# Three reorderings at stage borders of a two-layer conv/attention block: the gate products of the convolution, the second stream's 1/rms, and the first block pair's last sums

## The chip, the cores and the metric

The kernel runs on one core of a Trainium2 chip. The metric is the time of one execution on the device in microseconds (us), lower is better; the median of several runs is given. The engines are named as in the profile: PE is TensorE (matmuls), PEld its weight loads, DVE is VectorE, ACT is ScalarE, POOL is GpSimd, SP is SyncE, which here only issues DMAs.

## The reference, cut to what matters

Two streams of 256 tokens each, the latent `x` and the context `ctx`, of width 1024, go through two layers. Each layer is: half a gated feed-forward net (FFN), a mixer, and half an FFN again, every one behind an RMS norm with a modulation (a scale and a shift, computed from a conditioning vector) and added back through a gate. Layer 0's mixer is a short convolution, layer 1's is grouped-query attention. After layer 1's mixer only the latent stream goes on.

```python
def _rms(t, g):
    t32 = t.astype(jnp.float32)
    y = t32 * lax.rsqrt(jnp.mean(t32 * t32, axis=-1, keepdims=True) + NORM_EPS)
    return y.astype(t.dtype) * g

def _modulate(t, g, shift, scale):
    return _rms(t, g) * (1 + scale) + shift

def _swiglu(h, w13, w2):
    gte, up = jnp.split(h @ w13, 2, axis=-1)
    return (jax.nn.silu(gte) * up) @ w2

def _short_conv_mixer(h, w_in, k, w_out):
    bgate, cgate, xv = jnp.split(h @ w_in, 3, axis=-1)
    return (bgate * _dwconv3(cgate * xv, k)) @ w_out
```

## The kernel before

Activations are kept transposed: width on the 128 partitions (eight tiles k of 128, `KT = 8`), tokens along the free dimension, the latent stream in columns 0 to 255 (called s = 0) and the context stream in columns 256 to 511 (s = 1). Products keep fp32 accuracy by splitting each operand into a high part and a low rest (`split`: ACT copies the high part, DVE subtracts), and `mm3` (L133) makes three matmuls of one product: high by high, high weight by low activation, low weight by high activation. A "product" below is one such matmul, as in the description of the change. Weights come by DMA as raw fp32 tiles (`load_raw`, eight buffers `wr`), and `load_w` splits them into halves of 1024 columns (`wh`, `wl`, four buffers each).

**FFN.** 22 pairs of a gate tile and an up tile (`pg`, `pu`) are worked off in three groups (`THIRDS` = 8, 7, 7), each followed by `project`, the multiplication with the second weight. In the FFNs with both streams most pairs are done by blocks (`Pair`, with `h.blk` tiles of class `Blocks`): a scheme in the manner of Strassen with seven block products instead of eight. It needs sums of activation blocks (`Blocks.sums`: T1 to T4, high and low parts `th`, `tl`) and of weight blocks (`Pair.sums`: S1 to S4). `Pair.sums(1)` makes a copy of a weight block (`split_far`), then the subtraction at L729 and the split into S3 and S4. The block products are called in five steps: `head` (A11, A12), `five` (S1 by T1), `six` (S2 by T2, S4 by a plain block), `seven` (S3 by T3), `four` (A22 by T4).

**The borders.** The norm needs the sum of squares over all 1024 rows, so it can only start when the last tile of the stage before is done. At the end of a stage, `project` therefore does tiles 6 and 7 stream by stream: first s = 0, then s = 1. What the norm of a stream has to do is put into a list `pending` by `tail_norm`, and `flush(n)` runs the first n entries at chosen places in the program. For s = 0 these are three entries, run inside `project`. For s = 1 it is one entry, `both_parts`: `rms_sum` (two PE products with ones, L270; a square root on ACT, L275; a reciprocal `ri` on DVE, L279), `rms_all` (two PE products with the identity, L288, that spread `ri` over all partitions), and then the eight tiles of the norm itself (`scaled`, L300, and the high and low parts). The next stage begins with products of s = 0 only, so that the norm of s = 1 runs beside them.

The three kinds of border that the change touches:

- FFN to convolution (once). The convolution has three groups of products, `pv`, `pc` (weights `wcx`) and `pb` (weights `wb`, the gate b). For its first output tile, m = 0, it goes stream by stream with k outermost, three groups for each k, and calls `flush()` behind the twelfth `mm3` (n == 11).
- Into an FFN with blocks (twice: layer 0's second FFN and layer 1's first). Two plain pairs come first: pair 0 with s = 0, `flush()`, the load of pair 1's weights, pair 1 with s = 0, then `h.sums(0)`, pair 0 with s = 1, `h.sums(1)` and the first block pair's `sums(0)`, pair 1 with s = 1, the first block pair's `head`, `h.sums(2)` (T3 and T4), and the first block pair's `sums(1)` (S3 and S4). `tc.issue_after(every[-1])` keeps pair 1's products on PE behind the last product of `rms_all`.
- FFN to attention (once): a `flush()` between two projections.

**Order of instructions.** Outside the parts that are written out by hand, a planner sorts each engine's instructions before the run. It walks through time with its own estimates of durations, and when several instructions of an engine are ready it takes the one that stands first in the program. So the order in the program is a priority, not the order on the engine; a lower one is taken where the higher is not ready by the planner's estimate. `issue_after` adds a fixed order on one engine. On the chip each engine then follows the sorted order.

Of the kernel before, what the change touches and what calls it, by code (L numbers as in the profile page):

```python
# [18 lines left out]
KT = D // P  # L19
S = 256  # L20
# [27 lines left out]
def hybrid_kernel(ctx: ExitStack, tc: tile.TileContext, a: dict, out: bass.AP):  # L48
    nc = tc.nc
# [83 lines left out]
    def mm3(ps, w, m, first, last, more=False):  # L133
        wh, wl = w
        kw = {"skip_group_check": True} if more else {}
        mh, ml = m
        nc.tensor.matmul(ps, wh, mh, start=first, stop=False, **kw)  # L137
        nc.tensor.matmul(ps, wh, ml, start=False, stop=False, **kw)  # L138
        nc.tensor.matmul(ps, wl, mh, start=False, stop=last, **kw)  # L139

    def mm_wide(ps, ws, ms, first, last):

# [202 lines left out]
    class Early:  # L345
# [3 lines left out]
        w = S + 2  # L349
# [126 lines left out]
    pending = []  # L476

    def flush(n=9):
        while pending and n:
            pending.pop(0)()  # L480
            n -= 1
# [30 lines left out]
    def tail_norm(l, j, h):  # L512

        box = {}

        def tail(m, c0, c1):
            square_add(m, c0, c1)
            if m == KT - 1:
                if not box:
                    box["A"] = scale_of(l, j)  # L520
                    box["B"] = mod_ready(l, 3 * j)
                s = c0 // S

                def inv():
                    return rms_inv(s)

                def rest(part, ri, ks=range(4)):

                    if isinstance(h, Blocks):
                        h.block(s, part, box["A"], box["B"], ri, s == 0, ks)  # L530
                    else:
                        for k in ks:
                            norm_k(s, 4 * part + k, h, box["A"], box["B"], ri)

                def both_parts():
                    ri = inv()
                    for part in range(2):
                        rest(part, ri)

                if s == 0:  # L540
                    keep = []

                    def one():
                        keep.append(inv())
                        rest(0, keep[0])

                    pending.append(one)
                    pending.append(lambda: rest(1, keep[0], range(2)))
                    pending.append(lambda: rest(1, keep[0], range(2, 4)))
                else:  # L550
                    flush()
                    pending.append(both_parts)

        return tail

# [85 lines left out]
    def at13(j, k):  # L641

        return (k // 4) * 1024 + j * T2 + (k % 4) * P

    def w13_mm(pp, w, h, ks, c0, c1):
        for k in ks:
            mv = pick(h, k, c0, c1)
            for i in range(2):
                mm3(pp[i][:, c0:c1], w(at13(1 - i, k)), mv, k == 0, k == KT - 1)

    def w13_post(pp, g, c0, c1):
        n = c1 - c0
# [119 lines left out]
    def ffn(l, b, h, tot, gate, tail, gs=(), ev=(0, 0), z=None):  # L772
        gs = list(gs)
        i0 = 0
        for t, n in enumerate(THIRDS):
            between = ()
            if tot == T2:
                heads = []
                if t == 0 and not gs:

                    w = [load_w(a["w13"][l, b, 0])]
                    gs = [new_pair("g") for _ in range(2)]
                    pp = [(psum("pg"), psum("pu")) for _ in range(2)]
                    w13_mm(pp[0], w[0], h, range(KT), 0, S)
                    flush()
                    w.append(load_w(a["w13"][l, b, 1]))
                    with tc.issue_after(every[-1]):
                        w13_mm(pp[1], w[1], h, range(KT), 0, S)
                    h.sums(0)
                    w13_mm(pp[0], w[0], h, range(KT), S, T2)  # L790
                    w13_post(pp[0], gs[0], 0, T2)
                    heads.append(Pair(a["w13"][l, b, 2], h))
                    h.sums(1)
                    heads[0].sums(0)
                    w13_mm(pp[1], w[1], h, range(KT), S, T2)
                    w13_post(pp[1], gs[1], 0, T2)
                    heads[0].head()
                    h.sums(2)
                    heads[0].sums(1)
                prev = None  # L800
                for i in range(len(gs), n):
                    if t == 0 and not heads and i in AS_IS[l, b]:
                        w = load_w(a["w13"][l, b, i])
                        pp = psum("pg"), psum("pu")
                        if prev:
                            prev.seven()
                        if "T1" not in h.t:
                            with tc.issue_after(rows["W1"]):
                                h.sums()
                        w13_mm(pp, w, h, range(4), 0, T2)  # L810
                        if prev:
                            gs.append(new_pair("g"))
                            prev.four(gs[-1])
                            prev = None
                        w13_mm(pp, w, h, range(4, KT), 0, T2)
                        gs.append(new_pair("g"))
                        tick(3, w13_post(pp, gs[-1], 0, T2))
                        continue
                    if heads:
                        pr = heads.pop(0)  # L820
                    else:
                        pr = Pair(a["w13"][l, b, i0 + i], h)
                        pr.sums(0)
                        pr.sums(1)
                        pr.head()
                    pr.five()
                    at = prev.seven().ins if prev else None
                    pr.six()
                    if prev:
                        gs.append(new_pair("g"))  # L830
                        prev.four(gs[-1])
                    prev = pr
                    if i:
                        tick(0.9, at)

                def last():
                    gs.append(new_pair("g"))
                    prev.four(gs[-1])

                between = (prev.seven, last) if prev else ()  # L840
            else:
                for i in range(n):
                    w = load_w(a["w13"][l, b, i0 + i])
                    gs.append(beside(gp.tile([P, T2], F32R, name=nm("gx"), tag="gh")))
                    pp = psum("pg"), psum("pu")
                    if i0 + i < EARLY:
                        for k in range(KT):
                            for j in range(2):
                                ps = pp[j][:, : z.w]
                                mm3(ps, w(at13(1 - j, k)), z.at(k), k == 0, k == KT - 1)  # L850
                            if i == 0 and k == KT // 2:
                                flush(1)
                        if i < 3:
                            flush(1)
                        early_post(pp, gs[i], z.ri)
                        tick(1)
                        continue
                    for j in range(2):
                        ws = [w(at13(1 - j, k)) for k in range(KT)]
                        mm_wide(pp[j], ws, [h.both(k) for k in range(KT)], True, True)  # L860
                    beside_post(pp, gs[i])
                    tick(1)
            i0 += n

            def ws2(m):
                src = a["w2a"][l, b, m // 2] if t == 0 else a["w2b"][l, b, t - 1, m // 2]
                o = (m % 2) * n * P
                raw = load_raw(src[:, o : o + n * P], n * P)
                hi, lo = half()
                split(hi[:, : n * P], lo[:, : n * P], raw[:, : n * P])  # L870
                return lambda k: (hi[:, k * P : k * P + P], lo[:, k * P : k * P + P])

            cur = gs
            end = t == len(THIRDS) - 1
            project(
                ws2,
                (lambda k, c0, c1: cur[k]) if tot == S
                else lambda k, c0, c1: (cur[k][0][:, c0:c1], cur[k][1][:, c0:c1]), n,
                gate, tail if end else None, tot, 2 if end and tot == T2 else 0, ev[end], between,
            )  # L880
            gs = []
# [191 lines left out]
    h = hn  # L1073

    zs = []
    for m in range(KT):
# [4 lines left out]
        for c0, c1 in ((0, S), (S, T2)) if m == 0 else ((0, T2),):  # L1081
            groups = ((pv, wcx, P), (pc, wcx, 0), (pb, wb, (m % 2) * P))
            if m == 0:
                order = [(k, *g) for k in range(KT) for g in groups]
            else:
                order = [(k, *g) for g in groups for k in range(KT)]
            for n, (k, ps, w, off) in enumerate(order):
# [397 lines left out]
```

## Time and profile before

| | |
|---|---|
| median of 3 runs | 1556.71 us (1556.70 to 1556.72) |
| the profiled execution | 1558.75 us; its span, first to last instruction, 1557.0 us |
| PE busy | 1545.5 us, 99% of the span, 10252 matmuls |
| DVE, ACT, POOL busy | 82%, 50%, 14% |
| granted TensorE clock, mean | 0.999 |
| DMA | 263.5 MB, 169 GB/s mean |

The profiled execution took 2.04 us more than the median, and 1.75 us of it lie outside the span. PE is the engine that sets the end: what matters are the places where it stood still. A matmul's end in the profile is modelled, and neighbours overlap: a matmul over 256 columns has a duration of 0.28 us, while the next one starts 0.12 us after it. So the loss at a wait is read from the starts: the distance of two starts less the usual distance.

### The profile page before, as it was taken

What the parts mean: (1) busy time and instruction counts of PE and PEld (TensorE: products, weight loads), DVE (VectorE), ACT (ScalarE), POOL (GpSimd) and SP (SyncE); (2) the same over time, 40 slices, a digit from 0 to 9 for tenths busy, and PEclk for the clock granted to TensorE, in tenths of its full rate; (3) what the DMA queues carried; (4) which work ended last, traced back from release to release, by engine and by line L of the source; (5) the groups of instructions that cost most, each with busy time, mean ns of one, the idle gap of its engine ahead of it and who ended that gap; (6) DMA issues with size and microseconds to landing.
All of it is one profiled execution on the core that took longest, in us unless ns stands there. A gap on an engine that the chain in (4) does not pass through costs nothing.

```text
span 1557.0 us, 26280 instructions
## 1 busy us (share of the span) xinstructions
PE 1545.5 (99%) x10252; PEld 1416.9 (91%) x10252; DVE 1284.5 (82%) x2003; ACT 781.9 (50%) x1297; POOL 221.8 (14%) x187
## 2 busy tenths in 40 slices
PE   9999999999999999999999999999999999999999
PEld 7898998998888899989999899989999899998888
DVE  5789799799987489978979888968978888898676
ACT  5642553544322366436446476436446455774553
POOL 0012212200000012032032012022042002300000
PEclk9999999999999999999999999999999999999999
DMA  9557477475565424655656634655767843266562
GB/s 368 197 167 197 115 186 203 111 199 166 187 204 178 115 62 121 207 142 146 199 149 153 205 77 123 203 156 133 220 183 169 263 158 122 92 237 221 170 196 75
DMA packets 88254, 263.53 MB, mean 169 GB/s; under 512 B 10817, under 2 KB 12609, under 8 KB 88129
## 3 DMA queue, kind: packets, MB, share of 16 engines
q1 hardware_dynamic: 69408, 230.72, 45.7%
q0 software_dynamic: 16128, 29.37, 11.3%
q10 hardware_dynamic: 2592, 1.76, 0.4%
q8 instruction: 80, 1.31, 0.3%
q14 instruction: 46, 0.37, 0.1%
HBM read 259.45 MB, written 1.05 MB: 167 GB/s over the span
## 4 chain that ended last, share of the span: by engine, by line
PE 96%; DVE 2%; ACT 1%; DMA 1%; issue 0%; POOL 0%; ACTq 0%; DVEq 0%; POOLq 0%
PE py L138 9%; PE py L137 9%; PE py L139 9%; PE p L137 7%; PE p L139 7%; PE p L138 7%; PE q L137 5%; PE q L139 5%; PE q L138 5%; PE py L145 2%; PE pu L145 2%; PE pg L145 2%; PE py L147 1%; PE pg L147 1%; PE pu L147 1%; PE pv L137 1%
## 5 line engine op out<-in xcount | busy, mean ns | idle before, releaser
L108 ACT ACTIVATE wh<-wr 128x1024 fp32r<-128x1024 f32 (+2 forms) x446 | 394.7, 913 | 338.0 <-PE py L138 128.1
L109 DVE TENSOR_TENSOR wl<-wr,wh 128x1024 fp32r<-128x1024 f32 (+2 forms) x446 | 456.5, 1048 | 84.3 <-ACT wh L108 64.7
L178 DVE CUSTOM_DVE_ANT_0 junk<-wr,scbc,modb 128x1024 bf16<-128x1024 f32 x213 | 274.5, 1289 | 8.7 <-DMA wr<-in_modT 6.9
L138 PE MATMUL py<-gl,wh 128*128 128x512 f32 (+1 forms) x570 | 213.4, 374 | 0.0
L137 PE MATMUL py<-gh,wh 128*128 128x512 f32 (+1 forms) x570 | 213.3, 374 | 0.0
L139 PE MATMUL py<-gh,wl 128*128 128x512 f32 (+1 forms) x570 | 212.9, 373 | 0.0
L699 POOL TENSOR_SCALAR wr<-wr 128x512 f32<-128x512 f32 x56 | 101.3, 1809 | 542.4 <-DMA wr<-in_w 292.2
L562 DVE SCALAR_TENSOR_TENSOR x<-py,mod,x 128x256 f32<-128x256 f32 x213 | 94.2, 478 | 66.5 <-PE py L139 55.0
L137 PE MATMUL p<-th,wh 128*128 128x256 f32 x448 | 126.8, 283 | 0.0
L139 PE MATMUL p<-th,wl 128*128 128x256 f32 x448 | 126.8, 283 | 0.0
L138 PE MATMUL p<-tl,wh 128*128 128x256 f32 x448 | 126.8, 283 | 0.0
L139 PEld LDWEIGHTS py<-gh,wl 128*128 128x128 f32 x570 | 107.3, 188 | 19.3
L137 PEld LDWEIGHTS py<-gh,wh 128*128 128x128 f32 x570 | 107.4, 188 | 18.3
L138 PEld LDWEIGHTS py<-gl,wh 128*128 128x128 f32 x570 | 107.4, 188 | 18.0
L115 POOL DMA_DIRECT2D w4l<-in_w x56 | 54.1, 966 | 445.2 <-ACT w4l L114 423.6
L137 PE MATMUL q<-bh,wh 128*128 128x256 f32 x320 | 90.8, 284 | 0.8 <-ACT wh L108 0.8
L139 PE MATMUL q<-bh,wl 128*128 128x256 f32 x320 | 90.8, 284 | 0.0
L138 PE MATMUL q<-bl,wh 128*128 128x256 f32 x320 | 90.5, 283 | 0.0
L138 PEld LDWEIGHTS p<-tl,wh 128*128 128x128 f32 x448 | 86.0, 192 | 0.3
L137 PEld LDWEIGHTS p<-th,wh 128*128 128x128 f32 x448 | 86.0, 192 | 0.3
L139 PEld LDWEIGHTS p<-th,wl 128*128 128x128 f32 x448 | 86.0, 192 | 0.0
L759 ACT ACTIVATE sg<-sg 128x512 f32<-128x512 f32 x56 | 35.4, 632 | 90.9 <-DVE sg L758 90.6
(303 smaller groups left out, 4060.4 us busy)
## 6 DMA issues: line engine op xcount, KB each, us to landing
wr<-in_w SPq DMA_DIRECT2D x120, 512.0 KB, 4.8
wr<-in_modT SPq DMA_DIRECT2D x117, 512.0 KB, 4.7
wr<-in_w2b SPq DMA_DIRECT2D x64, 448.0 KB, 4.0
wr<-in_w2a SPq DMA_DIRECT2D x32, 512.0 KB, 4.5
wr<-in_w SPq DMA_DIRECT2D x56, 256.0 KB, 3.9
wr<-in_w POOLq DMA_DIRECT2D x56, 256.0 KB, 5.9
w4l<-in_w POOLq DMA_DIRECT2D x56, 256.0 KB, 6.0
pm<-in_mod SPq DMA_DIRECT2D x16, 512.0 KB, 10.2
```

The costliest lines, as they stand in the source:

```text
L108: nc.scalar.activation(out=hi, in_=src, func=AF.Copy)
L109: return nc.vector.tensor_tensor(out=lo, in0=src, in1=hi.bitcast(F32), op=ALU.subtract)
L115: nc.gpsimd.dma_start(out=lo, in_=src, accum_op=ALU.add)
L137: nc.tensor.matmul(ps, wh, mh, start=first, stop=False, **kw)
L138: nc.tensor.matmul(ps, wh, ml, start=False, stop=False, **kw)
L139: nc.tensor.matmul(ps, wl, mh, start=False, stop=last, **kw)
L145: nc.tensor.matmul(ps, w[0], m[2], start=first and n == 0, stop=False)
L147: nc.tensor.matmul(ps[:, :S], w[1], m[0], start=False, stop=last and n == len(ms) - 1)
L178: nc.vector.tensor_tensor_reduce(out=junk, in0=raw, in1=scbc[:, v, :], scale=0.5 if ch in (2, 8) else 1.0, scalar=modb[:, l, col : col + 1 ...
L562: ins = nc.vector.scalar_tensor_tensor(out=x[:, m, s * S : s * S + S], in0=ps[:, o : o + S], scalar=g[:, m, s : s + 1], in1=x[:, m, s * S ...
L699: nc.gpsimd.tensor_scalar(out=r1[:, :T2], in0=r2[:, :T2], scalar1=-1.0, scalar2=None, op0=ALU.mult)
L759: nc.scalar.activation(out=self.sg, in_=self.sg, func=AF.Silu)
```

## The change

- `mm3`, `w13_mm`: they return the last matmul, so that others can be ordered behind it. No instruction is added.
- `tail_norm`: the one entry for s = 1 becomes two. The first is `rms_sum`, the second (`turn`) is `rms_all` and the norm's eight tiles.
- The first two pairs of an FFN with blocks: `flush(1)` behind pair 0 runs `rms_sum` alone; then comes the load of pair 1's weights, then the products of pair 1 for the first two tiles k (12 matmuls), and behind the last of them on PE `turn`. The other 36 matmuls of pair 1 with s = 0 stay behind the last product of `rms_all`.
- The same place further on: the first block pair's `sums(1)` (S3, S4) stands ahead of `h.sums(2)` (T3, T4) in the program.
- Convolution, m = 0: `pv` and `pc` go over k as before, and `pb` follows four tiles later: the list has k = 0 to 4 of `pv` and `pc`, then one `pb` behind each further pair, and the last four `pb` at the end. `flush()` stays behind the twelfth entry, which is now `pv` of k = 5.

The other calls of `flush()` run both entries at once, in the order of before.

```diff
@@ mm3
-        nc.tensor.matmul(ps, wl, mh, start=False, stop=last, **kw)
+        return nc.tensor.matmul(ps, wl, mh, start=False, stop=last, **kw).ins
@@ tail_norm
-                def both_parts():
-                    ri = inv()
-                    for part in range(2):
-                        rest(part, ri)
-
+                keep = []
                 if s == 0:
-                    keep = []
...
                 else:
                     flush()
-                    pending.append(both_parts)
+
+                    def turn():
+                        ri = rms_all(*keep[0])
+                        for part in range(2):
+                            rest(part, ri)
+
+                    pending.append(lambda: keep.append(rms_sum(s)))
+                    pending.append(turn)
@@ w13_mm
             for i in range(2):
-                mm3(pp[i][:, c0:c1], w(at13(1 - i, k)), mv, k == 0, k == KT - 1)
+                ins = mm3(pp[i][:, c0:c1], w(at13(1 - i, k)), mv, k == 0, k == KT - 1)
+        return ins
@@ ffn
                     w13_mm(pp[0], w[0], h, range(KT), 0, S)
-                    flush()
+                    flush(1)
                     w.append(load_w(a["w13"][l, b, 1]))
+                    at = w13_mm(pp[1], w[1], h, range(2), 0, S)
+                    with tc.issue_after(at):
+                        flush()
                     with tc.issue_after(every[-1]):
-                        w13_mm(pp[1], w[1], h, range(KT), 0, S)
+                        w13_mm(pp[1], w[1], h, range(2, KT), 0, S)
                     h.sums(0)
...
                     heads[0].head()
+                    heads[0].sums(1)
                     h.sums(2)
-                    heads[0].sums(1)
@@ convolution, m == 0
             if m == 0:
-                order = [(k, *g) for k in range(KT) for g in groups]
+                order = [(k, *g) for k in range(KT) for g in groups[:2]]
+                for k in range(KT):
+                    order.insert(min(10 + 3 * k, len(order)), (k, *groups[2]))
```

## The prediction

> **What bounds the kernel now.** I read the page first, then PE's waits, then at each border the timelines of PE, ACT and DVE side by side. The page:
>
> ```profile
> span 1557.0 us, 26280 instructions
> PE 1545.5 (99%) x10252; PEld 1416.9 (91%) x10252; DVE 1284.5 (82%) x2003; ACT 781.9 (50%) x1297; POOL 221.8 (14%) x187
> ```
>
> PE is busy for 1545.5 of 1557.0 us, so all its idle time together is 11.5 us. The change adds and removes no matmul; it can only win or lose at places where PE stands still. PE's waits at the borders that it touches (us in total, times, longest):
>
> ```profile
> PE pv L137 <- ACT hh L310: 1.4, 1, 1.4
> PE q L137 <- ACT wh L108: 0.8, 2, 0.4
> PE ss L288 <- DVE ri L279: 0.7, 1, 0.7
> PE pg L137 <- ACT bh L392: 0.5, 1, 0.5
> PE pg L138 <- DVE bl L393: 0.4, 2, 0.2
> ```
>
> Together 3.8 us, a quarter of a per cent of the span. The loss is somewhat larger, because after a wait the distance of two starts is longer for a moment. So the change is worth a few us at most in either direction, and 0.2% (3.1 us), about what a measurement of this kernel can tell from no change, is near the top of what it can bring.
>
> **The change part by part: S3 and S4 ahead of T3 and T4 (two borders).** The wait of `q` is for S4's high part. The first of the two borders, in the timelines of PE, ACT and DVE:
>
> ```profile
> 591.29 0.28 PE L139 MATMUL p<-th,wl 128*128 128x256 f32 x1
> 591.96 0.38 PE L137 MATMUL q<-bh,wh 128*128 128x256 f32 x1 [0.39 <-ACT wh L108]
> 592.18 0.28 PE L138 MATMUL q<-bl,wh 128*128 128x256 f32 x1
> 592.30 0.30 PE L137 MATMUL p<-th,wh 128*128 128x256 f32 x1
> ...
> 593.44 0.28 PE L137 MATMUL q<-bh,wh 128*128 128x256 f32 x1
> ```
>
> ```profile
> 590.85 1.06 ACT L108 ACTIVATE wh<-wr 128x1024 fp32r<-128x1024 f32 x1 [0.31 <-DVE wr L729]
> ```
>
> ```profile
> 586.72 2.35 DVE L109 TENSOR_TENSOR tl<-hr,th 128x1024 fp32r<-128x1024 f32 x2
> ...
> 589.60 1.22 DVE L729 TENSOR_TENSOR wr<-wr,wr 128x1024 f32<-128x1024 f32 x1
> ```
>
> DVE finishes T3's and T4's low parts (two splits in 2.35 us), then one small split, then L729 at 589.60; ACT's split for S3 and S4 follows (590.85 to 591.91), then PE at 591.96. What L729 reads comes from L721, which stands ahead of the `tl` splits on DVE already (it is part of `sums(0)`). With the higher place in the program L729 goes ahead of the two `tl` splits at the latest, at 586.72 instead of 589.60, 2.88 us earlier, and the wait is gone with over 2 us to spare. What PE gains: products start 0.12 us apart (592.18 to 592.30), so the next after 591.29 would be due at 591.41. From 591.96 on, seven products start ahead of the one at 593.44; undisturbed they take 7 x 0.12 = 0.84 us, and it would start at 592.25. So 593.44 - 592.25 = 1.19 us are lost, because the low parts of the same tile are late too. The waits row has the same wait twice (0.8 us in two), once at each border, so I take 2 x 1.19 = 2.4 us. Late next could be T3 and T4, with L729 and the split of S3 and S4 ahead of them on DVE, 1.22 us each: their low parts end at 586.72 + 2.35 + 2.44 = 591.5, ahead of the first product with T3 at 592.30. If that cover were gone, a T3 product would wait by tenths. `sums(1)` also moves two copies on ACT and a DMA on POOL's queue (`split_far`):
>
> ```profile
> 545.82 0.87 POOL L115 DMA_DIRECT2D w4l<-in_w  x1 [6.67 <-ACT w4l L114]
> ```
>
> For this pair they run some 40 us ahead of the border already, so they cost nothing; SP has no part in `sums(1)`. Bounds: 2.4 us, or nothing if the sorted queue on DVE keeps L729 where it is.
>
> **1/rms behind 12 products (the same two borders).** First border, PE and DVE:
>
> ```profile
> 566.40 0.38 PE L138 MATMUL pg<-bl,wh 128*128 128x256 f32 x1 [0.22 <-DVE bl L393]
> ...
> 566.86 0.28 PE L139 MATMUL pu<-bh,wl 128*128 128x256 f32 x1
> 567.83 0.71 PE L288 MATMUL ss<-ident,ri 128*128 128x128 f32 x4 [0.69 <-DVE ri L279]
> 568.30 0.36 PE L137 MATMUL pg<-bh,wh 128*128 128x256 f32 x1
> ...
> 574.25 0.28 PE L138 MATMUL pg<-bl,wh 128*128 128x256 f32 x1
> ```
>
> ```profile
> 567.62 0.16 DVE L279 RECIPROCAL ri<-rs 128x2 f32<-128x2 f32 x1
> ...
> 572.47 1.22 DVE L109 TENSOR_TENSOR bl<-hr,bh 128x1024 fp32r<-128x1024 f32 x1
> ```
>
> Pair 0's last product starts at 566.86; the next is due at 566.98, but PE waits for `ri` until 567.83: 0.85 us lost. In the new order 12 products of pair 1 stand there, 12 x 0.12 = 1.44 us, and `rms_all` comes at 568.42, when `ri` (done 567.78) is there. The wait goes. Late next is the norm behind it. From the start of `rms_all` to the end of the low part `bl` of s = 1's first half it takes 572.47 + 1.22 - 567.83 = 5.86 us on DVE and ACT; PE first uses that tile at 574.25, 0.56 us later. In the new order the tile is ready at 568.42 + 5.86 = 574.28, while only 36 products instead of 48 stand between: PE arrives at 568.42 + 0.47 (568.30 less 567.83) + 36 x 0.12 = 573.21, and stands. So the 0.85 us come back as a wait six us later. What is left is what the planner can put into that wait: products that need only high parts, up to four (a gate and an up product of either pair) where one stood before 574.25. That is 3 x 0.12 = 0.36, less 0.10 for the restart (591.96 to 592.18 is 0.22 instead of 0.12) and 0.03 for the later tile: a gain of 0.23.
>
> Second border:
>
> ```profile
> 915.49 0.39 PE L137 MATMUL pg<-bh,wh 128*128 128x256 f32 x1 [0.52 <-ACT bh L392]
> ...
> 917.51 0.61 PE L288 MATMUL ss<-ident,ri 128*128 128x128 f32 x4
> ...
> 923.83 0.28 PE L138 MATMUL pg<-bl,wh 128*128 128x256 f32 x1
> ```
>
> ```profile
> 922.04 1.22 DVE L109 TENSOR_TENSOR bl<-hr,bh 128x1024 fp32r<-128x1024 f32 x1
> ```
>
> Here PE does not wait for `ri`, so the 12 products only push `rms_all` back, to 918.95, and the tile from 923.26 to 924.70, where it was used at 923.83: 0.87 lost, less 0.36 plus 0.10 as above, -0.61 us. Against that PE waits twice just ahead for s = 0's last tiles (0.52 us here and the second of the two waits for `bl`, 0.2 us, in the waits rows), and the 12 products are free to fill that where their weights are split in time. If they fill all 0.72 us, `rms_all` is at 918.23, the tile at 923.98, and the border gains 0.36 - 0.15 - 0.10 = 0.11. I take the middle, -0.25. Sum of both borders: 0.0. Bounds: -1.1 (no product moves into any wait: -0.13 and -0.97) and +2.1 (every wait ahead of `rms_all` filled, restarts included, and the norm in time: 0.85 + 0.32 + 0.92).
>
> Whether a product passes a late one matters here. At 566.40 a `pg` product waits 0.22 us for `bl` and none goes ahead of it. [...]
>
> **The lag of the b products (one border).** ACT, then PE, then the share of the engines in the first stream's pass, then DVE:
>
> ```profile
> 380.71 1.06 ACT L108 ACTIVATE wh<-wr 128x1024 fp32r<-128x1024 f32 x1 [1.66 <-PE py L138]
> 381.68 1.29 ACT L310 ACTIVATE hh<-t,mod 128x256 fp32r<-128x256 f32 x3
> ```
>
> ```profile
> 382.22 0.39 PE L137 MATMUL pv<-hh,wh 128*128 128x256 f32 x1 [1.43 <-ACT hh L310]
> ```
>
> ```profile
> 382.30:391.90 9.60, 9.60 (x80) 9.49 (x81) 9.26 (x22) 4.21 (x12) 0.00 (x0) 1.00 0.26 95
> ```
>
> ```profile
> 388.03 0.89 DVE L311 SCALAR_TENSOR_TENSOR hl<-t,mod,hh 128x256 fp32r<-128x256 f32 x2
> ```
>
> The wait of 1.43 us comes from ACT's queue: a weight split (380.71) stands ahead of the first norm tile. Everything up to there comes earlier in the program than the reordered products, and its relative order is the same, so I expect the same queue and the same wait. From 382.22 on PE has no idle time (9.60 of 9.60), so the lag has nothing to win there. It can lose: v and c alone use up a tile k in 6 products, 0.72 us, instead of 9, 1.08 us, and DVE, which makes the tiles, is busy for 9.26 of the 9.60 us. The tile k = 6 is ready at 388.03 + 0.89/2 = 388.47; in the new written order its low product is the 44th and due at 382.22 + 43 x 0.12 = 387.38, 1.1 us too early. But the b products of k = 1 to 4 are ready by then and free to fill. I take 0. Bounds: -1.1 in either pass, so -2.2 for both (queue as written), and +1.4 (the first norm tile gets ahead of the split). In the `flush()` there and the one ahead of the attention both entries run at once, as before: nothing.
>
> **Sum.** 2.4 + 0.0 + 0.0 = 2.4 us. The profiled execution took 1558.75 us, of which 1557.0 are the span; it becomes 1556.35 with a span of 1554.6. It stands 2.04 us above the median of 1556.71, which becomes 1554.3.
>
> **The rivals.** B: the waits ahead of `rms_all` are filled and the norm is not late, since the planner sorts the norm's DVE work differently: another 2.1 us, 1552.2. For it: the planner does take lower products where higher ones are late (`p` at 592.30 among `q`). Against it: 5.86 us of norm against 4.8 us of PE work. C: the first norm tile of the convolution passes the weight split: 1.4 us more, 1552.9. Against it: nothing in the change touches the two instructions. D, slower than before: PE arrives earlier at tiles that are made no faster. Place: the tile k = 6 in both passes of the convolution (-2.2) and the s = 1 tile at both block borders (-1.1); it decides as soon as the queue keeps the written order, and is then 3.3 us, 0.9 more than S3 and S4 bring: 1557.6. [...] Against it: the trace's queue already fills. E: the sorted queues place L729 as before, so that the change does nothing at its main place: 1556.7.
>
> **How the numbers follow.** My forecast, 1554.3, gets 0.52, with a spread of about 1 us either way; B 0.18, C 0.10, D 0.12, E 0.08. The range 1552.6 to 1557.6 holds the forecast, C, D, E and part of B. Faster by over 0.2% (below 1553.6): B, C and the lower end of the forecast, 0.34. Slower by over 0.2% (above 1559.8) takes more than D's full price, 0.06. The rest, 0.60, lies within.
>
> **What would show it.** Right: the row `PE q <- ACT wh` is gone, L729 stands ahead of the two `tl` rows; no wait for `ri` at the first block border, but waits for `bl` (L109) at the start of s = 1's pass at both; the wait of `pv` for `hh` is still about 1.4. Wrong: `q` still waits; new idle time between 382 and 400, or at 574 and 924 of more than 1 us; or the `pv` wait gone.

## The result, and the profile after

| | before | after |
|---|---|---|
| median of 22 runs | 1556.97 us (1556.3 to 1558.89) | 1554.24 us (1553.59 to 1556.77) |
| the profiled execution | 1558.75 us, span 1557.0 us | 1554.59 us, span 1552.8 us |

The ratio is 0.9982, with a 95% interval of 0.9975 to 0.9988. The forecast of 1554.3 us was right to 0.1 us. Its sum was right, two of its three terms were not: they were wrong in opposite directions. A hit this close is in part luck: the interval alone is a gain of 1.9 to 3.9 us, and the two medians here are 2.73 us apart, not 2.4: the median of before is 1556.97 in this series, where the forecast started from 1556.71.

The page of after, its first line and the engines; columns as before:

```profile
span 1552.8 us, 26276 instructions
PE 1544.5 (99%) x10252; PEld 1416.9 (91%) x10252; DVE 1283.3 (83%) x2003; ACT 783.6 (50%) x1297; POOL 221.1 (14%) x187
```

**Not all of the 4.2 us between the two spans belongs to the change.** After starts the convolution's first `pv` at 380.31, before at 382.22, 1.91 us later, and nothing that was edited takes effect ahead of that product. The windows of 14 to 18 us from the start, of before and then of after (stretch and its length, us; busy time and instructions of PE, PEld, DVE, ACT, POOL; granted clock; DMA share; GB/s):

```profile
14.00:18.00 4.00, 4.00 (x33) 2.58 (x37) 0.79 (x3) 1.28 (x4) 0.00 (x0) 0.57 1.03 418
```

```profile
14.00:18.00 4.00, 3.98 (x49) 2.67 (x39) 1.99 (x6) 2.03 (x6) 0.00 (x0) 1.00 1.03 415
```

Before had a granted clock of 0.57 there, after had 1.00. Two kernels of the experiments show 0.57 in this stretch as well and reach `pv` at 381.7 and 382.1; those without it, with the same code ahead of `pv`, reach it at 379.8 to 380.3 (hh_first and the kernels built on it change that code and are left out here). So single executions of the same kernel scatter by some 2 us, and each part is read below from distances within one trace.

**Where the rest came from.** Two distances hold all three edits. The first runs from the last product ahead of the convolution to the first one behind its gates; the second from the first gate product of the first FFN with blocks to the first score product of the attention, with both block borders in it. Their ends in after's timeline of PE:

```profile
378.60 0.28 PE L139 MATMUL py<-gh,wl 128*128 128x256 f32 x1
...
513.12 0.39 PE L137 MATMUL py<-zh,wh 128*128 128x512 f32 x1
...
558.52 0.28 PE L137 MATMUL pg<-bh,wh 128*128 128x256 f32 x1
...
1303.65 0.40 PE L137 MATMUL psc<-kh,qh 128*128 128x512 f32 x1
```

The convolution's distance is 134.51 (before 134.39, from 380.51 to 514.90): the lag costs 0.13, before rounding. That of the block borders is 745.14 (before 747.68, from 560.30 to 1307.98): 2.54 gained. From the first score product to the end there are 249.15 against 248.99. Together 2.25 us, which with the 1.91 of the start makes the 4.16 between the spans.

PE's waits after (us in total, times, longest):

```profile
PE pv L137 <- ACT hh L310: 1.4, 1, 1.4
...
PE pg L138 <- DVE bl L109: 0.8, 2, 0.4
```

The rows of `q` for `wh` and of `ss` for `ri`, and the waits of `pg` for the last tiles of s = 0, are gone. `pv` waits as before. New is `pg` for `bl` (L109), once at each block border.

**S3 and S4.** The first border in after's timelines of PE, DVE and ACT:

```profile
588.85 0.28 PE L139 MATMUL p<-th,wl 128*128 128x256 f32 x1
588.97 0.28 PE L137 MATMUL q<-bh,wh 128*128 128x256 f32 x1
...
590.65 0.28 PE L137 MATMUL q<-bh,wh 128*128 128x256 f32 x1
590.96 0.38 PE L139 MATMUL p<-bh,wl 128*128 128x256 f32 x1
591.18 0.28 PE L137 MATMUL p<-bh,wh 128*128 128x256 f32 x1
```

```profile
584.54 1.22 DVE L732 TENSOR_TENSOR wr<-wr,wr 128x1024 f32<-128x1024 f32 x1
...
589.80 1.10 DVE L109 TENSOR_TENSOR wl<-wr,wh 128x512 fp32r<-128x512 f32 x1
```

```profile
585.79 1.06 ACT L108 ACTIVATE wh<-wr 128x1024 fp32r<-128x1024 f32 x1
```

L732 is the L729 of before. It and ACT's split are done at 586.85, 2.1 us ahead of the `q` product that needs them, and `q` follows `p` after the usual 0.12 us. But at 590.96 a product stands 0.31 us behind its neighbour, and the next one 0.22: it needs the low part of a plain weight block of the next block pair (`p<-bh,wl`), which DVE has ready at 590.90 only.

**1/rms.** The first border, PE and DVE:

```profile
563.92 0.50 PE L270 MATMUL ss<-ones,acc 128*128 128x1 f32 x4
564.28 0.36 PE L137 MATMUL pg<-bh,wh 128*128 128x256 f32 x1
...
566.27 0.60 PE L288 MATMUL ss<-ident,ri 128*128 128x128 f32 x4
...
571.38 0.28 PE L137 MATMUL pu<-bh,wh 128*128 128x256 f32 x1
572.07 0.39 PE L138 MATMUL pg<-bl,wh 128*128 128x256 f32 x1 [0.41 <-DVE bl L109]
```

```profile
565.86 0.16 DVE L279 RECIPROCAL ri<-rs 128x2 f32<-128x2 f32 x1
...
569.66 1.22 DVE L418 TENSOR_TENSOR hr<-hr,hr 128x1024 f32<-128x1024 f32 x1
570.79 1.22 DVE L109 TENSOR_TENSOR bl<-hr,bh 128x1024 fp32r<-128x1024 f32 x1
```

`rms_all` starts 7.75 us behind the border's first gate product, where it was 7.53 before (567.83 less 560.30): with 12 more products ahead of it, 1.44 us of work, it is only 0.22 us later. At the second border it is 8.02 against 7.46. Then PE stands for `bl`: the next product after 571.38 was due at 571.50 and starts at 572.07. From the border's first gate product to the first product of the block pairs PE needs 24.69 us instead of 25.35 (first border) and 24.95 instead of 25.18 (second).

**The lag.** The pass of the first stream, in the windows of after from 380.40 to 390.00, and PE's timeline in it:

```profile
380.40:390.00 9.60, 9.60 (x80) 9.50 (x81) 9.24 (x22) 4.32 (x12) 0.00 (x0) 1.00 0.27 87
```

```profile
382.97 0.28 PE L137 MATMUL pc<-hh,wh 128*128 128x256 f32 x1
383.09 0.28 PE L138 MATMUL pb<-hl,wh 128*128 128x256 f32 x1
383.21 0.28 PE L139 MATMUL pb<-hh,wl 128*128 128x256 f32 x1
383.33 0.28 PE L137 MATMUL pb<-hh,wh 128*128 128x256 f32 x1
```

PE stays busy for all 9.60 us; where `pv` and `pc` run ahead of the tiles, `pb` products of earlier tiles fill in.

### The profile page after: what moved, and what is told of

Same layout as the page of the kernel before. It is cut to its first block, busy times and chain, and to the rows that moved or that the text cites. A ratio compares the mean times of both kernels' runs of the same rounds, so it can differ in the third digit from the quotient of the medians.

```text
span 1552.8 us, 26276 instructions
## 1 busy us (share of the span) xinstructions
PE 1544.5 (99%) x10252; PEld 1416.9 (91%) x10252; DVE 1283.3 (83%) x2003; ACT 783.6 (50%) x1297; POOL 221.1 (14%) x187
## 3 DMA queue, kind: packets, MB, share of 16 engines
HBM read 259.45 MB, written 1.05 MB: 168 GB/s over the span
## 4 chain that ended last, share of the span: by engine, by line
PE 97%; DVE 1%; ACT 1%; issue 0%; POOL 0%; DVEq 0%; ACTq 0%; POOLq 0%
PE py L138 9%; PE py L137 9%; PE py L139 9%; PE p L139 7%; PE p L138 7%; PE p L137 7%; PE q L139 5%; PE q L137 5%; PE q L138 5%; PE py L145 2%; PE pu L145 2%; PE pg L145 2%; PE py L147 1%; PE pg L147 1%; PE pu L147 1%; PE pv L137 1%
## 5 line engine op out<-in xcount | busy, mean ns | idle before, releaser
L109 DVE TENSOR_TENSOR wl<-wr,wh 128x1024 fp32r<-128x1024 f32 (+2 forms) x446 | 457.2, 1049 | 84.2 <-ACT wh L108 65.0
```

The costliest lines, as they stand in the source:

```text
L109: return nc.vector.tensor_tensor(out=lo, in0=src, in1=hi.bitcast(F32), op=ALU.subtract)
```

## The experiments

For each kernel the two distances above were read from PE's timeline: "blocks" from the first gate product of the first FFN with blocks to the first score product, "conv" across the convolution. Medians of the same chip job are side by side. The intervals of the ratios reach about 0.1% (1.4 us) to either side, so the medians do not rank the smaller parts; these are read from the distances, of one profiled execution for each kernel.

| kernel | median, us | before, us | ratio (95%) | blocks, us | conv, us |
|---|---|---|---|---|---|
| before | 1556.97 | | | 747.68 | 134.39 |
| after | 1554.24 | 1556.97 | 0.9982 (0.9975–0.9988) | 745.14 | 134.51 |
| s4_only | 1555.61 | 1556.77 | 0.9990 (0.9981–0.9999) | 746.47 | 134.39 |
| rms_only | 1555.12 | 1556.77 | 0.9991 (0.9982–1.0000) | 745.94 | 134.39 |
| lag_only | 1556.79 | 1556.77 | 0.9996 (0.9987–1.0005) | 747.69 | 134.51 |
| rms_24 | 1559.99 | 1556.77 | 1.0012 (1.0003–1.0021) | 749.46 | 134.51 |
| bl_first | 1553.09 | 1556.72 | 0.9978 (0.9968–0.9988) | 743.95 | 134.51 |
| hh_first | 1553.23 | 1556.72 | 0.9980 (0.9971–0.9989) | 745.00 | 133.81 |
| hh_first_nolag | 1553.55 | 1556.72 | 0.9977 (0.9968–0.9986) | 745.10 | 133.69 |
| t4_late | 1553.92 | 1556.72 | 0.9983 (0.9974–0.9992) | 744.84 | 134.49 |
| rms_6 | 1553.77 | 1556.80 | 0.9979 (0.9970–0.9988) | 744.54 | 134.51 |
| all_lag | 1551.95 | 1556.80 | 0.9966 (0.9953–0.9978) | 743.50 | 133.81 |
| all_nolag | 1551.64 | 1556.80 | 0.9967 (0.9956–0.9979) | 743.52 | 133.69 |

**One part alone: s4_only.** Before, with one edit:

```diff
                     heads[0].head()
+                    heads[0].sums(1)
                     h.sums(2)
-                    heads[0].sums(1)
```

> The kernel before with one part of the change alone: S3 and S4 ahead of T3 and T4. Theory 1 (the terms as the two traces show them): the wait of q for the weight split goes at both block borders, and PE, from the first head product on, is 0.83 us earlier at each, 1.66 us together; the borders ahead of that (rms_all) stay as before; the time is 1555.3 against 1557.0. Theory 2 (the term as the prediction sized it): 1.19 us at each border, 2.4 together, 1554.6, with the missing part in the whole change lost to an interplay of the parts. Theory 3: the parts need each other, and alone this one gains under 0.5 us, because the products behind are not there earlier.

The blocks lost 1.21 us, 0.6 for each border, and all of it behind the first product of the block pairs (from that product to the 300th behind it 36.58 instead of 37.19). That is half of the 1.19 of the prediction's term, and less than the first theory's 1.66 for both. `q`'s wait for S4 is gone here too; late next are `q` products of the next pair, S1 by T1 (timelines of PE and ACT of s4_only):

```profile
593.53 0.28 PE L139 MATMUL q<-bh,wl 128*128 128x256 f32 x1
593.84 0.39 PE L137 MATMUL q<-th,wh 128*128 128x256 f32 x1
594.07 0.28 PE L138 MATMUL q<-tl,wh 128*128 128x256 f32 x1
```

```profile
592.73 1.06 ACT L108 ACTIVATE wh<-wr 128x1024 fp32r<-128x1024 f32 x1
```

0.31 and 0.23 us where 0.12 is usual. The high part of that pair's weight is done on ACT at 593.79 only. So the term's size fell, its mechanism stands: PE ran on to the next late weight.

**One part alone: rms_only.** After, with the old order of the convolution and of the sums:

```diff
                     heads[0].head()
-                    heads[0].sums(1)
                     h.sums(2)
+                    heads[0].sums(1)
@@ conv, m == 0
+                order = [(k, *g) for k in range(KT) for g in groups]
```

> The kernel before with one part of the change alone: the second stream's 1/rms behind 12 products of pair 1. Theory 1 (the two traces): 0.65 us gained at the first block border and 0.23 at the second, 0.9 together, 1556.1; PE does not wait for ri, but waits about 0.4 us for the second stream's low part at the start of its pass at both borders. Theory 2 (the prediction): 0.0 together, 1557.0, with the same waits. Theory 3 (the wait for ri was all that mattered): 0.85 at the first border and none at the second, and no new wait.

The blocks lost 1.74 us. 0.67 of it is at the first border's norm and 0.24 at the second's, just as in after (0.65 and 0.23); that is the 0.9 of the first theory. The other 0.41 at each border, which no theory had, lies at S4, which this kernel does not touch. Its timeline of DVE:

```profile
586.18 1.22 DVE L109 TENSOR_TENSOR tl<-hr,th 128x1024 fp32r<-128x1024 f32 x1
...
588.02 1.22 DVE L732 TENSOR_TENSOR wr<-wr,wr 128x1024 f32<-128x1024 f32 x1
589.16 1.22 DVE L109 TENSOR_TENSOR tl<-hr,th 128x1024 fp32r<-128x1024 f32 x1
```

On DVE L732 runs between the two `tl` splits, although the program has it behind both. The parts are not independent: 1.21 and 1.74 make 2.95, after gained 2.54. What S4 brought in after, 0.83 for each border, includes 0.41 that the new 1/rms order brings by itself.

**One part alone: lag_only.** Before, with the lagged `order` of the convolution alone.

> The kernel before with one part of the change alone: the lag of the b products in the convolution's first tile. Theory 1 (the two traces and the prediction): nothing; the first pv product waits 1.43 us for the high part as before, and from it to the first product of the next projection PE needs within 0.15 us of 132.68 us as before. Theory 2: the lag alone wins up to 1.4 us at the first pv. Theory 3: the 1.9 us by which the first pv came earlier in the changed kernel's trace belong to the change; then it comes at 380.3 here as well and the time falls by as much. By theory 1 those 1.9 us are the scatter of the start-up.

The convolution's distance is 134.51, as in after, 0.13 us more than before; the rest is as before (747.69). The ratio's interval holds 1. So the lag is a small loss, and its price does not hang on the other parts.

**How far 1/rms can be pushed back: rms_24 and rms_6.** After, with 24 or 6 products of pair 1 ahead of `turn` instead of 12:

```diff
-                    at = w13_mm(pp[1], w[1], h, range(2), 0, S)
+                    at = w13_mm(pp[1], w[1], h, range(4), 0, S)      # rms_6: range(1)
...
-                        w13_mm(pp[1], w[1], h, range(2, KT), 0, S)
+                        w13_mm(pp[1], w[1], h, range(4, KT), 0, S)   # rms_6: range(1, KT)
```

> The changed kernel with 24 products of pair 1 ahead of rms_all instead of 12, 24 behind. Theory 1 (behind rms_all the norm of the second stream is what PE waits for): rms_all comes up to 1.44 us later at either border and the second stream's low part as much later, so the wait for it grows from 0.4 to about 1.7 us at both borders, and the time is 2 to 2.9 us longer than the changed kernel's, 1556.3 to 1557.1. Rival (what counted was PE's idle time ahead of rms_all, the norm is hidden): the same time as the changed kernel, 1554.2.

PE's waits of rms_24:

```profile
PE pg L138 <- DVE bl L109: 2.1, 2, 1.1
...
PE pg L137 <- ACT bh L108: 1.1, 2, 0.5
```

`rms_all` is 1.41 and 1.44 us later than in after, and these are 12 products of 0.12: each of them is paid for later. At the first border the kernel loses 1.40 us (26.09 against 24.69), so with everything ahead of `rms_all` full, a product more is a product lost. That confirms the wait for `bl` as the place where the late norm is paid. At the second border it loses 2.94 us (27.89 against 24.95), twice as much, from the same two waits. There the granted clock fell to 0.50; the section on the hardware shows it. The expected time of 1556.3 to 1557.1 did not reckon with that: of the eleven runs only the two fastest lie in it.

> The changed kernel with 6 products of pair 1 ahead of rms_all instead of 12. Theory 1 (what counts behind the border is when rms_all starts; the products ahead of it are worth having only as far as they fill PE's idle time): at the first border rms_all cannot start ahead of ri and comes about 0.2 us earlier than with 12, at the second about 0.5 us earlier; the waits of 0.41 us for the low part shrink by as much, 0.3 to 0.7 us gained together, 1553.7. Rival (the number of products ahead of rms_all only has to cover the wait for ri, less is a loss): PE waits for ri again at the first border, 0.3 us or more lost, 1554.6.

The blocks lost another 0.60 us against after. PE's waits of rms_6 have no row for `bl` any more, but one for `ri`:

```profile
PE ss L288 <- DVE ri L279: 0.4, 1, 0.4
```

At the first border the wait for `ri` gives back what the earlier norm gains (24.65 against 24.69); at the second border, where `ri` is ready in time, six products less ahead of `rms_all` gain 0.50 (24.45 against 24.95). What counts is how early `rms_all` can start, and twelve products were more than there was time to fill.

**The wait for `bl` taken away: bl_first.** In after's queue L418, the first subtraction of `h.sums(0)`, stands on DVE ahead of the `bl` split that PE waits for (569.66 and 570.79 above). Here the sums are ordered behind that split:

```diff
@@ Blocks.block
-                split(hi, lo, raw)
+                self.lows.append(split(hi, lo, raw).ins)
@@ the first two pairs
-                    h.sums(0)
+                    with tc.issue_after(h.lows[0]):
+                        h.sums(0)
```

> The changed kernel with one order added on DVE: the first subtraction for T1 (L418) stands behind the low part of the second stream's first half instead of ahead of it. Theory 1 (at both block borders PE waits at the start of the second stream's pass for that low part, which stands behind L418 on DVE): the part is ready about 0.57 us earlier, the waits of 0.41 us go, and each border gains about 0.5 us, 1.0 together: from the first gate product of the first border to the first score product 744.1 us in the trace instead of 745.1, the time 1553.2. Rival (the wait only moves on, to the second half's low part or to T1): under 0.4 us together.

DVE and PE of bl_first:

```profile
570.10 1.23 DVE L109 TENSOR_TENSOR bl<-hr,bh 128x1024 fp32r<-128x1024 f32 x1 [0.52 <-ACT bh L108]
...
571.63 1.22 DVE L418 TENSOR_TENSOR hr<-hr,hr 128x1024 f32<-128x1024 f32 x1
```

```profile
571.22 0.28 PE L137 MATMUL pu<-bh,wh 128*128 128x256 f32 x1
571.38 0.39 PE L138 MATMUL pg<-bl,wh 128*128 128x256 f32 x1
```

The wait shrank from 0.41 to less than the profile lists, and the blocks lost 1.19 us against after, 0.54 at each border's norm. So the new wait was not the price of the twelve products alone: a subtraction whose result PE did not need yet stood ahead of the split.

**The wait of `pv`: hh_first and hh_first_nolag.** Ahead of the first norm tiles ACT splits the weight of `pb`. Here that weight is loaded in two halves, and the second half is split behind the third high part of the norm; hh_first_nolag has the old order of the convolution besides.

```diff
@@ norm_k: the high part's instruction is kept
+        highs.append(nc.scalar.activation(out=hh, in_=t, func=AF.Identity, bias=b).ins)
@@ conv, m == 0
+            halves = [load_w(a["cw_b"][0][:, :1024], 1024)]
+            with tc.issue_after(highs[2]):
+                halves.append(load_w(a["cw_b"][0][:, 1024:], 1024))
```

> The changed kernel with one order added on ACT at the convolution: the second half of the b weights is split behind the third high part of the norm instead of ahead of the first. Theory 1 (the 1.43 us ahead of the first pv product come from that split standing ahead of the high part in ACT's queue): the wait goes down to 0.2 us or less, and the first product of the next projection comes 1.0 to 1.4 us earlier, counted from the last product ahead of the convolution; the time 1553.0. Rival (the low parts on DVE are as late as the high parts): the wait at pv goes, but PE waits after its first three products instead, and the gain is under 0.5 us.

ACT of hh_first, and its row among PE's waits:

```profile
378.05 1.31 ACT L312 ACTIVATE hh<-t,mod 128x256 fp32r<-128x256 f32 x3 [1.34 <-DVE t L300]
379.27 1.05 ACT L108 ACTIVATE wh<-wr 128x1024 fp32r<-128x1024 f32 x1
```

```profile
PE pv L137 <- ACT hh L312: 0.2, 1, 0.2
```

The wait went from 1.43 to 0.17 us, so the order of the two on ACT was its cause. But the convolution took only 0.70 us less, between the 1.0 to 1.4 of the first theory and the rival's 0.5. Of 1.27 us at its start 0.57 is given back: 0.12 behind the first three products, which the low parts hold up, and 0.45 at the start of the second stream's pass, where PE now comes ahead of that stream's first tiles (products at 388.58, 388.80, 389.22 and 389.45).

> The kernel of hh_first with the b products back in their old place beside v and c, so that hh_first and this one differ in the lag alone. Theory 1 (the lag moves nothing that PE waits for): both within 0.2 us in the trace, this one the earlier by the 0.13 us that the lag cost without hh_first. Rival (the lag pays once the first high part is there, since the later split of the second b half is then what the b products wait for): this one 0.5 to 1.2 us slower than hh_first.

The convolution takes 133.69 us, 0.12 less than with the lag: the lag does not help even where PE starts earlier. The medians have the two the other way round (1553.55 against 1553.23), which is within their scatter. No trace shows a gain from the lag.

**The late weight block: t4_late.** After, with T4's split (`keep("T4", b21)`) put off until the next pair's `sums(1)` has been issued, to let DVE reach that pair's low parts earlier.

```diff
@@ Blocks.sums(2)
-                keep("T4", b21)
+                self.last = lambda: keep("T4", b21)
@@ the block pairs, behind pr.sums(1)
+                        if h.last:
+                            h.last()
+                            h.last = None
```

> The changed kernel with T4's split moved in the program behind the weight sums of the second block pair, which puts one split less on DVE ahead of that pair's A11 low part. Theory 1 (what is left of the loss at S4, 0.36 us at each border, is A11's low part of the next pair, queued on DVE behind T4's split): PE loses nothing there, 0.3 to 0.36 us gained at each border, 0.7 together: 744.4 us instead of 745.1 between the marks named above. Rival (A11's low part is late for another reason, its high part on ACT): no change, or a loss where T4 itself comes too late for the first A22 product.

The blocks lost 0.30 us against after. The late `p<-bh,wl` is gone; `q` products with T1 and the low part of the next pair's weight lose part of it a little later. The block was late because of T4's split ahead of it, but moving that brings less than half of the 0.7 that both borders still lost there, and less than the 0.6 to 0.7 expected. It is a small number: over the first 300 products of the block pairs t4_late needs 36.22 and 36.21 us, after 36.36 and 36.35, but the second border of hh_first, with after's order there, 36.22 as well. In the next two kernels, against bl_first, the gain is clearer (36.07 or 36.08 at both borders, against 36.29 and 36.31).

**Together: all_lag and all_nolag.** bl_first, hh_first and t4_late in one kernel, with the lag and without it.

> The changed kernel with the three orders of bl_first, hh_first and t4_late together. Theory 1 (the waits lie one behind the other on PE's path, so the gains add up): against the changed kernel's trace 0.70 us at the convolution, 1.19 at the two block borders and 0.30 at S4, 2.2 us together: 742.9 to 743.9 us from the first gate product of the first border to the first score product, 133.8 from the last product ahead of the convolution to the next projection; the time 1552.0. Rival (they share DVE, and one takes back what another gives): under 1.5 us together, 1552.8 or more.

> The kernel of all_lag with the b products of the convolution's first tile back in their old place. Theory 1 (the lag only costs): 0.12 us less at the convolution, else the same, 1551.9, the fastest of all. Rival: slower than all_lag.

Against after the three gains are 1.19, 0.70 and 0.30, together 2.19; all_lag has 1.64 less in the blocks and 0.70 less in the convolution, 2.34. They add up, at least; they lie at different places. all_nolag takes another 0.12 from the convolution and has the lowest median, 1551.64 us, 0.9967 (0.9956 to 0.9979) of before; runs do not tell it from all_lag (0.9966). Its page, where the share of PE rounds to 100%:

```profile
span 1549.4 us, 26280 instructions
PE 1543.1 (100%) x10252; PEld 1415.9 (91%) x10252; DVE 1284.2 (83%) x2003; ACT 781.6 (50%) x1297; POOL 219.4 (14%) x187
```

## Why the prediction was right, and where its steps were not

| step | forecast, us | measured, us |
|---|---|---|
| S3 and S4, two borders | 2.4 gained | 1.66 in after (1.21 alone) |
| 1/rms, first border | 0.23 gained | 0.65 gained |
| 1/rms, second border | 0.25 lost | 0.23 gained |
| the lag | 0 | 0.13 lost |
| sum | 2.4 gained | 2.4 gained |

**The level of the runs** was set by the forecast's 2.04 us between the profiled execution of before and its median, so that the forecast is the old median of 1556.71 less 2.4. The 2.04 us are no constant of the kernel: most of them belong to the slow start-up of that one execution, whose first `pv` came 1.91 us later than after's. After's profiled execution did not have it and stands 0.35 us above its own median.

**S3 and S4.** Right: the wait of `q` is gone, L732 stands ahead of the `tl` splits with over 2 us to spare for PE, and the cover for T3 and T4 held: the second `tl` split is done at 589.89 (it starts at 588.67), and the next product with a T tile behind it comes at 593.56. Wrong: the size. The step that failed is "late next could be T3 and T4". L732 and the split of S3 and S4 went ahead of other work on DVE too, not of T3 and T4 alone, and the low part of the next pair's plain block (589.80) came late instead. I had looked through what the two moved instructions pass, but not to the end of that queue. Besides, the 1.19 us held 0.41 that the 1/rms part takes away without this edit.

**1/rms.** The mechanism was right: the wait for `ri` goes, and a wait for `bl` at the start of the pass of s = 1 takes its place, with four products that need high parts only ahead of it (571.02 to 571.38 in PE's timeline). The size was wrong, by 0.42 and 0.48 us. I moved `rms_all` back by all twelve products, less the wait for `ri`: to 568.42 at the first border, 0.59 us behind its old place, and to the middle of 918.95 and 918.23, 1.08 behind, at the second. It came only 0.22 and 0.56 behind. I had let the products fill waits at the second border only, and there only half, though a wait of the same kind (`pg` for `bl`, L393) stood at the first border too, 566.40 in before's row. Some of the twelve ran among pair 0's last products, from 564.28 on. At the first border the wait at 566.40, where the distance of starts was 0.35 us too long, and the restart behind it, 0.10, are gone, less 0.08 for the change from the sums to products: 0.37, and by just that `rms_all` comes ahead of my figure (0.59 less 0.22). At the second border the products filled 0.88 of their 1.44 us, more than the 0.72 that I had as the most, again since the restarts go with the waits. The norm behind the first border was 0.12 us shorter as well, 5.74 us from `rms_all` at 566.27 to the end of `bl` at 572.01.

In the traces of before and after, PE's 10252 matmuls and DVE's 2003 instructions stand, by line and tile, in the order of the built kernel, so the products that filled PE's waits had their places in the sorted queue. What the runs refuted is D's premise, that the sorted queue keeps the written order.

**The lag.** Right: the wait of `pv` stayed at 1.43 us, PE stayed busy, and the `pb` products filled. The 0.13 us lost lie near the chosen 0 and far from the bounds of −2.2 and +1.4. Rival C, that the norm tile passes the weight split, did not happen; hh_first shows that it would have been worth 0.70 us, not 1.4, since later tiles then hold PE up.

**The rivals.** B (all waits filled, the norm in time) is half of what happened: the waits were filled and the norm was still late. bl_first shows that the rest of B was to be had by one more ordering on DVE (1.19 us on top of 0.88, where B had 2.1). E did not happen: L732 moved ahead of both `tl` splits.

So the sum is right because S4 was taken 0.7 too large and 1/rms 0.9 too small; no step of the prediction ties these two errors together, and that they cancel is luck. The bounds of each term held what was measured; the values chosen within them did not, the lag's aside. For S4 the choice was the upper bound itself.

## What to carry to other kernels

When an instruction moves up on a busy engine, the price can fall on a later entry of that engine's queue and not on the instructions that were passed on paper, as here on the next pair's plain block (0.31 us between two starts instead of 0.12): list the whole queue up to the next few products, with the time at which each result is needed. When independent products are put ahead of a late operation, count the small waits ahead of that place as room for them, each with its restart of 0.10 us (here that room was 0.37 us more than reckoned at the first border, 0.88 in all at the second); beyond that room the further products were paid in full (twelve more cost 1.40 us at the first border). Two edits on the same queue are not a sum: alone they gained 1.21 and 1.74 us, together 2.54.

## What the runs showed of the hardware that was not expected

**The clock halved behind two short waits.** rms_24 has the same two waits at both block borders, 0.54 and 1.05 us, ending 1.8 us apart. Its windows, two at the first border and two at the second:

```profile
570.62:574.03 3.41, 2.67 (x21) 2.26 (x19) 3.41 (x7) 3.38 (x8) 1.35 (x2) 1.00 0.19 32
574.03:577.44 3.41, 2.56 (x21) 2.56 (x22) 2.83 (x4) 2.37 (x4) 0.00 (x0) 1.00 0.25 45
922.19:925.60 3.41, 1.82 (x13) 1.42 (x12) 2.98 (x4) 2.40 (x5) 0.00 (x1) 1.00 0.46 77
925.60:929.02 3.42, 3.42 (x18) 3.42 (x17) 3.28 (x3) 2.11 (x3) 0.00 (x0) 0.50 0.02 5
```

At the first border the granted clock stayed at 1.00; behind the second border's waits it was 0.50 over 3.4 us. PE's timeline there:

```profile
923.04 0.39 PE L137 MATMUL pg<-bh,wh 128*128 128x256 f32 x1 [0.54 <-ACT bh L108]
...
924.83 0.39 PE L138 MATMUL pg<-bl,wh 128*128 128x256 f32 x1 [1.05 <-DVE bl L109]
...
926.10 0.41 PE L138 MATMUL pu<-bl,wh 128*128 128x256 f32 x1
926.31 0.41 PE L139 MATMUL pu<-bh,wl 128*128 128x256 f32 x1
```

From 925.6 on products start 0.21 us apart instead of 0.12. In the records of the clock the half speed lasts 3.41 us, from 925.60 to 929.02, and it explains the second border's additional 1.5 us (2.94 less 1.40): about 16 products start 0.09 us later each. In the same records every boundary inside the kernel (at 4.00, 14.24, 17.66, 925.60 and 929.02 us) lies a whole number of 3.413 us from the others: 3, 1, 266 and 1 times that from one to the next. In before's records the boundaries at 4.12, 14.36 and 17.77 us lie 10.24 and 3.413 us apart, 3 and 1 times the same. On that grid the windows above are cut. At the second border both waits fall into one of them, and PE stands idle for 1.59 of its 3.41 us; at the first border a boundary at 574.03 parts them, 0.74 and 0.85 us. Whether only the second border lost its clock for this reason is not shown: no run shifted the waits against the grid to test it. The longest gap ahead of the drop is 1.05 us, and idle time alone does not settle it: the wait of `pv`, 1.43 us within the window from 379.47 to 382.88 of the same trace, left the clock at 1.00, while in the start-up it fell behind a window with 1.06 us idle (10.83 to 14.24).

The runs of this kernel lie around 1556.9, 1558.4 and 1560.2 us, and their mean granted clocks step with them: 1.000, then 0.999, then 0.997 to 0.998. The drop and the start-up together would make such steps, since 3.41 us at half the clock take 0.001 off the mean over 1558 us, but only one execution was profiled.

**The same in the start-up.** Between 14 and 18 us the granted clock is 0.57 in the profiled executions of before, rms_only and rms_24, and 1.00 in the others. It, too, comes behind a wait that most of the others do not have. Among PE's waits in before:

```profile
PE ss L270 <- DVE acc L263: 1.6, 1, 1.6
```

The wait ends at 13.04 us, the slow stretch begins at 14.36 and lasts to 17.77. In rms_only it is 0.9 us and in rms_24 1.1; of the ten without the slow stretch only lag_only has it, with 0.7. The three reach the convolution 1.4 to 2.5 us after the others with the same code, most of what the executions of one kernel differ by, and about as much as the change itself brings.

**A restart cost about 0.1 us beside the wait.** The distance of the first two starts behind a wait was 0.22 us instead of 0.12 (572.07 to 572.29 in after); the forecast's 0.10 for it held.
